# A scaled matmul with an added matrix: rows mapped to tiles in blocks of 1024 in place of one block of 8192

## The chip, the cores and the metric

The kernel runs on one NeuronCore of a Trainium2 chip. The other cores are not used by it. The metric is the device time of one execution in microseconds (us), a median over several runs. The profile is of one execution and reports times from the first to the last instruction (the span), which is shorter than the device time.

## What is computed

```python
# x: (16, 512, 1024) float32, weight: (1024, 768) float32, add_value: (16, 512, 768) float32
def reference(x, weight, scale, add_value):          # scale = 0.1
    return (scale * np.matmul(x, weight) + add_value).astype(np.float32)
```

Flattened, x has 8192 rows of 4 KB, add_value and the output have 8192 rows of 3 KB. The rows are independent of each other, so the kernel may treat them in any order, as long as x, add_value and the output use the same one.

## The kernel before

**Tiles.** The 8192 rows are worked on as 64 tiles of 128 rows, one row in each of the 128 partitions. Which row goes to which tile is set by three views, `x_v`, `add_v` and `out_v` (lines 54 to 56): partition p owns the 64 neighbouring rows 64p to 64p+63, and tile t takes row 64p+t of each partition. One transfer of n tiles therefore reads, in each partition, one unbroken run of n rows (4 KB each for x, 3 KB for add_value and the output); the runs of neighbouring partitions lie 64 rows apart in memory, which is 256 KB for x and 192 KB for the others. The weight has a view of its own, `w_v`: partition p of a transfer takes one 3 KB row, and neighbouring partitions lie two rows, 6 KB, apart.

**The order of transfers.** All transfers are issued by SyncE (SP) in the order of the list `STREAM`, written out by hand. An entry is an operation, a first tile and a number of tiles: `x` loads x (line 241), `w` one of eight weight pieces (line 93), `a` loads add_value (line 247), `o` stores output tiles (line 255), `l` and `r` the left and right part of the last tile. One loop at the end of the kernel walks this list; it also decides when the compute of a tile is recorded, by calling `step()` where a transfer needs room or finished tiles.

**Buffers.** `xs` holds 24 tiles of x (tile t in slot t mod 24). `ao` holds 24 tiles: add_value is loaded into a slot, the result is written over it in place, and the output is stored from it. So `x` of tile t waits until tile t-24 was cast, `o` waits for the last result in it, and `a` of tile t waits until the output of tile t-24 has landed in memory. In the beginning `ao` also holds the weight pieces and the first three products.

**The compute of one tile.** GpSimd (POOL) casts a tile of x to bf16 (line 129). TensorE (PE) transposes it with four matmuls against an identity (line 139), ScalarE (ACT) copies the result out of PSUM (line 145), and PE multiplies it with the eight weight pieces in 16 matmuls (line 161). VectorE (DVE) computes scale times product plus add_value in one instruction (`finish`, line 169). Nine pairs of tiles (`PAIRS`) go another way: GpSimd casts them seven steps ahead (`cast_pair`, line 102), and VectorE transposes them in place of TensorE (`turn_pair`, line 113). Three PSUM buffers (`mm_pool`) take the products, so TensorE can be up to three tiles ahead of VectorE.

**The beginning.** Ten dummy matmuls warm TensorE (line 87). Tiles 0 to 2 are multiplied with the weight pieces as these arrive (`head`); their products are put aside, and add_value is added when it is there (`added`, line 228). Tile 3 is prepared with them, and from tile 4 on the kernel is in its regular course: in `step()` for tile t, four of the eight weight pieces are multiplied, then tile t+1 is transposed, then the other four follow.

Of the kernel before, what the change touches and what calls it, by code (L numbers as in the profile page):

```python
# [11 lines left out]
STREAM = [  # L12
    ("x", 0, 1), ("x", 1, 1), ("x", 2, 1), ("w", 0, 1), ("w", 1, 1), ("w", 2, 1),
    ("w", 3, 1), ("w", 4, 1), ("w", 5, 1), ("x", 3, 1), ("w", 6, 1), ("w", 7, 1),
    ("a", 0, 3), ("x", 4, 4), ("a", 3, 1), ("a", 4, 4), ("x", 8, 4), ("x", 12, 4),
    ("a", 8, 8), ("x", 16, 8), ("a", 16, 8), ("x", 24, 8), ("o", 0, 8), ("o", 8, 8),
    ("a", 24, 4), ("x", 32, 4), ("a", 28, 8), ("a", 36, 4), ("x", 36, 8), ("o", 16, 8),
    ("x", 44, 4), ("a", 40, 8), ("x", 48, 4), ("o", 24, 8), ("x", 52, 8), ("a", 48, 4),
    ("o", 32, 8), ("a", 52, 4), ("a", 56, 8), ("x", 60, 4), ("o", 40, 8), ("o", 48, 8),
    ("o", 56, 4), ("o", 60, 2), ("o", 62, 1), ("l", 63, 1), ("r", 63, 1),  # L20
]

# [10 lines left out]
def kernel(  # L33
# [8 lines left out]
    nc = tc.nc  # L42
    P = 128
# [3 lines left out]
    x_f = x.flatten_outer_dims()  # L47
    add_f = add_value.flatten_outer_dims()
    out_f = out.flatten_outer_dims()
    M, K = x_f.shape  # L50
    _, N = weight.shape
    T = M // P
    KC = K // (2 * P)
    KJ = 2 * KC
    CUT = 512

    x_v = x_f.rearrange("(p t) k -> p t k", p=P)
    add_v = add_f.rearrange("(p t) n -> p t n", p=P)
    out_v = out_f.rearrange("(p t) n -> p t n", p=P)

    w_v = weight.rearrange("(c p r) n -> p c r n", p=P, r=2)

# [10 lines left out]

    zeros = const.tile([P, CUT], bf16, name="zeros")
    nc.vector.memset(zeros, 0.0)  # L75
    identity = const.tile([P, P], fp32, name="identity")
    make_identity(nc, identity)
    xs = const.tile([P, X_SLOTS, K], fp32, name="xs")
    ao = const.tile([P, A_SLOTS, N], fp32, name="ao")
# [6 lines left out]
    for _ in range(WARM):  # L86
        nc.tensor.matmul(warm[:, 0:CUT], zeros[:, 0:P], zeros, start=True, stop=True)  # L87

    def load_w(j, n):

        s = A_SLOTS - KJ + j
        if n == 1:
            nc.sync.dma_start(ao[:, s, :], w_v[:, j // 2, j % 2, :])  # L93
        else:
            nc.sync.dma_start(ao[:, s:s + 2, :], w_v[:, j // 2, :, :])
        for i in range(n):
            nc.vector.tensor_copy(w_bf[:, j + i, :], ao[:, s + i, :])  # L97
# [7 lines left out]
    def turn_pair(t0, a):  # L105

        if a == 0:
            vt = vt_pool.tile([P, 2, KC, P], fp32, tag="vt")
            vt_tiles[t0] = vt
# [23 lines left out]
    def transpose(t, pieces=1):  # L133
        cast_to(t)

        pairs = xb_tiles.pop(t).bitcast(fp32)
        tp = tp_pool.tile([P, KC, P], fp32, tag="tp")
        for c in range(KC):
            nc.tensor.transpose(tp[:, c, :], pairs[:, c * P:(c + 1) * P], identity)  # L139
        xt = xt_pool.tile([P, KJ, P], bf16, tag="xt")  # L140
        src = tp.bitcast(bf16).rearrange("p c (m r) -> p c r m", r=2)
        dst = xt.rearrange("p (c r) m -> p c r m", r=2)
        q = KC // pieces
        for c in range(0, KC, q):
            nc.scalar.copy(dst[:, c:c + q, :, :], src[:, c:c + q, :, :])  # L145
# [18 lines left out]

    BOTH = [(0, CUT), (CUT, N)]

# [8 lines left out]
    def head(op, s, n):  # L175


        for i in range(s, s + n):
            if op == "x" and i < EARLY:
                transpose(i, 2)  # L180
                have_x.append(i)
                for j in have_w:
                    product(i, j, BOTH)
            elif op == "w":
                if i == KJ - 1:
                    transpose(EARLY)
                have_w.append(i)
                for t in have_x:
                    product(t, i, BOTH)
        if len(have_w) == KJ and len(have_x) == EARLY and not done["step"]:  # L190
            for t in range(EARLY):

                if t == 1:
                    nc.scalar.mul(  # L194
                        ao[:, EARLY_AT + t, :], mm_tiles[t, BOTH[0]][:, 0:N], float(scale))
                else:
                    nc.vector.tensor_scalar(  # L197
                        ao[:, EARLY_AT + t, :], mm_tiles[t, BOTH[0]][:, 0:N], float(scale), None,
                        op0=mybir.AluOpType.mult)
            done["step"] = EARLY  # L200
# [3 lines left out]
    def step():  # L204
        t = done["step"]
        if t < T - 1:
            for j in range(KJ):
                if j == KJ // 2:
                    if t + 1 not in in_pair:
                        transpose(t + 1)  # L210
                    cast_to(min(t + 2, done["x"] - 1))
                    if t + 7 in PAIRS:
                        cast_pair(t + 7)
                product(t, j, BOTH)
            finish(t, BOTH[0], 0, N)
            for a in range(P // 32):
                if t + 6 - a in PAIRS:
                    turn_pair(t + 6 - a, a)
        else:
            for cols in BOTH:  # L220
                for j in range(KJ):
                    product(t, j, [cols])
                finish(t, cols, *cols)
        done["step"] += 1

    def added(t):
        assert done["step"] >= EARLY
        nc.vector.tensor_add(  # L228
            ao[:, t, :], ao[:, EARLY_AT + t, :], ao[:, t, :])

    for op, s, n in STREAM:
        last = s + n - 1
        if op == "w":
            load_w(s, n)
            head(op, s, n)
        elif op == "x":
            if last >= X_SLOTS:
                while done["cast"] <= last - X_SLOTS:
                    step()
            k = s % X_SLOTS  # L240
            nc.sync.dma_start(xs[:, k:k + n, :], x_v[:, s:s + n, :])  # L241
            done["x"] = s + n
            if last < EARLY:
                head(op, s, n)
        elif op == "a":
            k = s % A_SLOTS
            nc.sync.dma_start(ao[:, k:k + n, :], add_v[:, s:s + n, :])
            for t in range(s, min(s + n, EARLY)):
                added(t)
        else:  # L250
            while done["step"] <= last:
                step()
            k = s % A_SLOTS
            n0, n1 = {"o": (0, N), "l": (0, CUT), "r": (CUT, N)}[op]
            nc.sync.dma_start(out_v[:, s:s + n, n0:n1], ao[:, k:k + n, n0:n1])


# [33 lines left out]
```

## Time and profile before

| what | value |
|---|---|
| device time, median of 6 runs (lowest to highest) | 212.99 us (212.4 to 213.94) |
| the profiled execution: device time | 213.13 us |
| the profiled execution: span | 211.2 us |
| granted TensorE clock, mean | 0.977 |
| busy share of the span: PE, DVE, POOL, ACT | 93%, 62%, 30%, 23% |
| bytes read from memory, written to it | 61.87 MB, 25.17 MB |

The span and what lies around it (213.13 - 211.2 = 1.9 us) add up to the device time of that execution. A busy share is an average over the whole span; it doesn't say by itself which engine sets the end. For that one has to look at what each waits for, in the stages where it waits. A transfer is seen twice in the profile: the instruction on SP that issues it, and the time from there to its landing, which includes the time that it stands in the queue behind earlier transfers. The 16 DMA engines each carry a sixteenth of every transfer, and a transfer has landed when the last of the 16 is done.

### The profile page before, as it was taken

The numbers are of one execution on the slowest core, as the hardware profiler recorded it, in microseconds if no ns is written. First come the engines' busy times: TensorE is split into PE (matmuls) and PEld (weight loads), VectorE is DVE, ScalarE is ACT, GpSimd is POOL, SyncE is SP. The second block draws the span as 40 slices with busy tenths as digits, with TensorE's granted clock in tenths as the row PEclk, the third lists the DMA queues.
The fourth block names the chain that finished last, engine by engine and source line by source line (L and its number), as shares of the span: only waits on it lengthen the run. The fifth ranks groups of instructions, "written<-read, shape, count | busy, mean of one in ns | idle before, by whom it ended". The sixth has DMA issues, their size and how long they took to land.

```text
span 211.2 us, 3032 instructions
## 1 busy us (share of the span) xinstructions
PE 197.1 (93%) x1218; PEld 120.2 (57%) x1218; DVE 131.2 (62%) x223; ACT 49.2 (23%) x52; POOL 63.8 (30%) x69
## 2 busy tenths in 40 slices
PE   7877299999999999999999999999999999999980
PEld 2544255666566666666565666655666666666650
DVE  1447113229979689699599596986983994223330
ACT  3503013322303103113023031021130230332310
POOL 1310423551080080720900714407208230152000
PEclk9999759999999999999999999999999999999997
DMA  6999999999999999999999999999999999999993
GB/s 237 409 413 446 406 431 428 450 450 394 451 442 399 424 437 433 419 431 427 446 438 420 433 410 447 413 433 447 420 404 440 417 406 436 361 437 441 412 410 118
DMA packets 6781, 87.22 MB, mean 413 GB/s; under 512 B 752, under 2 KB 880, under 8 KB 2928
## 3 DMA queue, kind: packets, MB, share of 16 engines
q1 hardware_dynamic: 6768, 87.03, 97.7%
q8 instruction: 9, 0.15, 0.3%
q14 instruction: 4, 0.03, 0.0%
HBM read 61.87 MB, written 25.17 MB: 412 GB/s over the span
## 4 chain that ended last, share of the span: by engine, by line
PE 85%; DMA 10%; SPq 1%; POOL 0%; ACT 0%; issue 0%; DVE 0%; POOLq 0%; ACTq 0%
PE mm L161 76%; PE tp L139 9%; DMA xs<-in_x_dram 7%; DMA ao<-in_weight_dram 3%; SPq L241 1%; POOL xb L129 0%; ACT xt L145 0%; SPq L93 0%; DVE ao L169 0%; POOLq L129 0%; ACTq L145 0%
## 5 line engine op out<-in xcount | busy, mean ns | idle before, releaser
L161 PE MATMUL mm<-w_bf,xt 128*128 128x512 bf16 (+1 forms) x736 | 130.8, 331 | 1.9 <-DVE w_bf L97 1.3
L161 PEld LDWEIGHTS <-xt 128*128 128x128 bf16 x736 | 69.4, 99 | 52.4 <-ACT xt L145 11.0
L169 DVE SCALAR_TENSOR_TENSOR ao<-mm,ao 128x768 f32<-128x768 f32 (+2 forms) x62 | 58.6, 944 | 60.1 <-PE mm L161 49.8
L145 ACT COPY xt<-tp 128x1024 bf16<-128x1024 bf16 (+1 forms) x49 | 46.5, 963 | 150.3 <-PE tp L139 150.3
L113 DVE STREAM_TRANSPOSE vt<-vx 32x256 f32<-32x256 f32 x144 | 62.7, 436 | 3.1 <-POOL vx L102 0.9
L129 POOL CAST xb<-xs 128x1024 bf16<-128x1024 f32 x43 | 43.6, 1045 | 45.5 <-PE tp L139 24.4
L161 PE MATMUL mm<-w_bf,vt 128*128 128x512 bf16 (+1 forms) x288 | 49.7, 326 | 0.0
L102 POOL CAST vx<-xs 128x1024 bf16<-128x1024 f32 x18 | 18.3, 1043 | 78.8 <-DVE vt L113 43.5
L161 PEld LDWEIGHTS <-vt 128*128 128x128 bf16 x288 | 28.2, 98 | 17.6
L139 PE MATMUL tp<-identity,xb 128*128 128x128 f32 x184 | 28.8, 282 | 5.2 <-POOL xb L129 4.8
L139 PEld LDWEIGHTS tp<-identity,xb 128*128 128x128 f32 x184 | 22.6, 146 | 11.5 <-POOL xb L129 5.2
L97 DVE CAST w_bf<-ao 128x768 bf16<-128x768 f32 x8 | 4.5, 564 | 4.7 <-DMA ao<-in_weight_dram 4.7
L87 PE MATMUL warm<-zeros 128*128 128x512 bf16 x10 | 4.4, 631 | 1.2 <-DVE zeros L75 1.2
L125 DVE CAST xb<-xs 128x512 bf16<-128x512 f32 x3 | 1.3, 427 | 4.9 <-DMA xs<-in_x_dram 4.9
L87 PEld LDWEIGHTS <-zeros 128*128 128x128 bf16 x10 | 1.3, 143 | 3.4 <-issue 2.2
L127 POOL CAST xb<-xs 128x512 bf16<-128x512 f32 x2 | 1.7, 868 | 4.7 <-DMA xs<-in_x_dram 4.7
L228 DVE TENSOR_TENSOR ao<-ao 128x768 f32<-128x768 f32 x3 | 2.7, 951 | 0.0
L197 DVE TENSOR_SCALAR ao<-mm 128x768 f32<-128x768 f32 x2 | 1.8, 952 | 1.0 <-PE mm L161 1.0
L127 ACT ACT_TABLE_LOAD x1 | 1.3, 1283 | 0.7 <-PEq L272 0.7
L127 ACT CAST xb<-xs 128x512 bf16<-128x512 f32 x1 | 0.6, 619 | 2.3 <-DMA xs<-in_x_dram 2.3
L194 ACT ACTIVATE ao<-mm 128x768 f32<-128x768 f32 x1 | 0.8, 816 | 0.0
L75 DVE MEMSET zeros<- 128x256 uint32 x1 | 0.3, 272 | 0.9 <-PEq L272 0.9
(6 smaller groups left out, 0.9 us busy)
## 6 DMA issues: line engine op xcount, KB each, us to landing
out_dram<-ao SPq DMA_DIRECT2D x7, 3072.0 KB, 23.7
xs<-in_x_dram SPq DMA_DIRECT2D x4, 4096.0 KB, 33.5
ao<-in_add_value_dram SPq DMA_DIRECT2D x5, 3072.0 KB, 15.8
xs<-in_x_dram SPq DMA_DIRECT2D x7, 2048.0 KB, 16.9
ao<-in_add_value_dram SPq DMA_DIRECT2D x5, 1536.0 KB, 16.5
ao<-in_weight_dram SPq DMA_DIRECT2D x8, 384.0 KB, 7.4
xs<-in_x_dram SPq DMA_DIRECT2D x4, 512.0 KB, 4.8
out_dram<-ao SPq DMA_DIRECT2D x1, 1536.0 KB, 12.1
```

The costliest lines, as they stand in the source:

```text
L87: nc.tensor.matmul(warm[:, 0:CUT], zeros[:, 0:P], zeros, start=True, stop=True)
L97: nc.vector.tensor_copy(w_bf[:, j + i, :], ao[:, s + i, :])
L102: nc.gpsimd.tensor_copy(vx[:, i, :], xs[:, (t0 + i) % X_SLOTS, :])
L113: nc.vector.transpose(vt[b:b + 32, :, 32 * a:32 * a + 32], pairs[32 * a:32 * a + 32, :, b:b + 32])
L127: other(xb[:, K // 2:K], src[:, K // 2:K])
L129: nc.gpsimd.tensor_copy(xb, src)
L139: nc.tensor.transpose(tp[:, c, :], pairs[:, c * P:(c + 1) * P], identity)
L145: nc.scalar.copy(dst[:, c:c + q, :, :], src[:, c:c + q, :, :])
L161: nc.tensor.matmul(mm_tiles[t, cols[0]][:, n0:n1], lhs(t, j), w_bf[:, j, n0:n1], start=(j == 0), stop=(j == KJ - 1))
L169: nc.vector.scalar_tensor_tensor(a, mm_tiles[t, part][:, n0:n1], float(scale), a, op0=mybir.AluOpType.mult, op1=mybir.AluOpType.add)
L228: nc.vector.tensor_add(ao[:, t, :], ao[:, EARLY_AT + t, :], ao[:, t, :])
L241: nc.sync.dma_start(xs[:, k:k + n, :], x_v[:, s:s + n, :])
```

## The change

Three things change. First, the views: rows are grouped in 8 blocks of 1024. In a block, partition p owns 8 neighbouring rows, and tile t of the 64 takes row `1024*(t//8) + 8*p + t%8`. A transfer of 8 tiles covers one unbroken stretch of memory (4 MB of x, 3 MB of the others); one of 4 tiles reads or writes half of each partition's 8 rows. Inside a partition the run is as long as before for the same number of tiles. Neighbouring partitions now lie 32 KB (x) and 24 KB (the others) apart.

Second, a helper `rows` picks a block and tiles in it, and refuses a transfer that crosses a block's border. Third, since some entries of `STREAM` crossed such borders, the list is written anew: where transfers of 8 tiles began at a tile that is not a multiple of 8, they are moved or split, and the order around them differs. The number of entries, 47, and the bytes are the same.

```diff
 STREAM = [
     ("x", 0, 1), ("x", 1, 1), ("x", 2, 1), ("w", 0, 1), ("w", 1, 1), ("w", 2, 1),
     ("w", 3, 1), ("w", 4, 1), ("w", 5, 1), ("x", 3, 1), ("w", 6, 1), ("w", 7, 1),
-    ("a", 0, 3), ("x", 4, 4), ("a", 3, 1), ("a", 4, 4), ("x", 8, 4), ("x", 12, 4),
-    ("a", 8, 8), ("x", 16, 8), ("a", 16, 8), ("x", 24, 8), ("o", 0, 8), ("o", 8, 8),
-    ("a", 24, 4), ("x", 32, 4), ("a", 28, 8), ("a", 36, 4), ("x", 36, 8), ("o", 16, 8),
-    ("x", 44, 4), ("a", 40, 8), ("x", 48, 4), ("o", 24, 8), ("x", 52, 8), ("a", 48, 4),
-    ("o", 32, 8), ("a", 52, 4), ("a", 56, 8), ("x", 60, 4), ("o", 40, 8), ("o", 48, 8),
+    ("a", 0, 3), ("a", 3, 1), ("x", 4, 4), ("x", 8, 4), ("a", 4, 4), ("x", 12, 4),
+    ("a", 8, 8), ("x", 16, 8), ("a", 16, 8), ("x", 24, 8), ("o", 0, 8), ("x", 32, 8),
+    ("a", 24, 4), ("a", 28, 4), ("o", 8, 8), ("x", 40, 4), ("a", 32, 8), ("o", 16, 8),
+    ("x", 44, 4), ("a", 40, 8), ("x", 48, 4), ("o", 24, 8), ("x", 52, 4), ("a", 48, 8),
+    ("x", 56, 4), ("o", 32, 8), ("x", 60, 4), ("a", 56, 8), ("o", 40, 8), ("o", 48, 8),
     ("o", 56, 4), ("o", 60, 2), ("o", 62, 1), ("l", 63, 1), ("r", 63, 1),
 ]
...
-    x_v = x_f.rearrange("(p t) k -> p t k", p=P)
-    add_v = add_f.rearrange("(p t) n -> p t n", p=P)
-    out_v = out_f.rearrange("(p t) n -> p t n", p=P)
+    G = 8
+
+    x_v = x_f.rearrange("(g p t) k -> p g t k", p=P, t=G)
+    add_v = add_f.rearrange("(g p t) n -> p g t n", p=P, t=G)
+    out_v = out_f.rearrange("(g p t) n -> p g t n", p=P, t=G)
+
+    def rows(view, s, n):
+        assert s // G == (s + n - 1) // G
+        return view[:, s // G, s % G:s % G + n, :]
...
-            nc.sync.dma_start(xs[:, k:k + n, :], x_v[:, s:s + n, :])
+            nc.sync.dma_start(xs[:, k:k + n, :], rows(x_v, s, n))
...
-            nc.sync.dma_start(ao[:, k:k + n, :], add_v[:, s:s + n, :])
+            nc.sync.dma_start(ao[:, k:k + n, :], rows(add_v, s, n))
...
-            nc.sync.dma_start(out_v[:, s:s + n, n0:n1], ao[:, k:k + n, n0:n1])
+            nc.sync.dma_start(rows(out_v, s, n)[:, :, n0:n1], ao[:, k:k + n, n0:n1])
```

The instructions on TensorE, VectorE, ScalarE and GpSimd are the same in kind, number and order; what differs there is which transfers they wait for.

## The prediction, made before the changed kernel ran

> **What bounds the kernel now.** I read the chain of waits first, then the DMA rows, then the stages one by one, because the first two seem to contradict each other. The page gives:
>
> ```profile
> DMA  6999999999999999999999999999999999999993
> GB/s 237 409 413 446 406 431 428 450 450 394 451 442 399 424 437 433 419 431 427 446 438 420 433 410 447 413 433 447 420 404 440 417 406 436 361 437 441 412 410 118
> q1 hardware_dynamic: 6768, 87.03, 97.7%
> PE 85%; DMA 10%; SPq 1%; POOL 0%; ACT 0%; issue 0%; DVE 0%; POOLq 0%; ACTq 0%
> ```
>
> The chain puts 85% on PE, yet the data queue keeps the 16 DMA engines busy for 97.7% of the span. The chain in order of time shows where each rules:
>
> ```profile
> 9.81 13.85 DMA xs<-in_x_dram
> ...
> 23.80 1.05 POOL xb L129
> ...
> 24.90 1.12 PE tp L139 x4
> 26.02 5.08 PE mm L161 x16
> ...
> 31.53 2.63 PE mm L161 x16
> ...
> 205.41 0.42 DVE ao L169
> ```
>
> The transfer of x tiles 4 to 7, issued at 9.81 and landed 13.85 later (23.66), frees GpSimd's cast and then PE at 24.90. From there PE runs almost without a hole until 205.4; the first tile takes 5.08 us, later ones 2.63 plus 0.44 of transposes. But the chain follows the last engine instruction, which ends at 205.8, and the span goes on to 211.2. The last 5.4 us belong to the output transfers. The stages in between, each row being busy times, then granted PE clock, DMA share, GB/s:
>
> ```profile
> 8.00:13.00 5.00, 4.84 (x31) 2.76 (x30) 2.88 (x6) 1.56 (x4) 0.00 (x0) 1.00 1.03 404
> 29.00:73.00 44.00, 44.00 (x281) 27.17 (x279) 27.74 (x47) 12.14 (x12) 13.10 (x13) 0.98 1.00 429
> 182.00:184.50 2.50, 2.50 (x18) 1.61 (x17) 0.39 (x2) 1.01 (x1) 0.00 (x0) 1.00 1.09 347
> 188.00:203.00 15.00, 15.00 (x99) 9.32 (x98) 4.44 (x6) 5.06 (x5) 3.27 (x4) 1.00 0.99 421
> 207.00:208.20 1.20, 0.00 (x0) 0.00 (x0) 0.00 (x0) 0.00 (x0) 0.00 (x0) 1.00 0.39 143
> 208.20:210.40 2.20, 0.00 (x0) 0.00 (x0) 0.00 (x0) 0.00 (x0) 0.00 (x0) 0.55 0.05 20
> ```
>
> The DMA engines are full from the first bytes to about 207. In the last 2.2 us they move at 20 GB/s with a share of 0.05, about one engine of 16: one straggler finishes alone, 2.2 us after the others. The end is set by the transfer stream, and in it by its slowest engine. PE stands just behind: the last store is issued at 205.87, the 15 other engines are through at about 208.1 (the 1.2 us from 207 at a mean share of 0.39), so 2.3 us pass from the last issue to their end, and PE could be about 2.2 us later before the straggler at 210.3 ceased to hide it.
>
> **What the Trainium skill says.** The page "DMA: Bandwidth & Descriptors", section "Bandwidth", puts the ceiling of the 16 engines' path at 435 GB/s; the trace's 429 in the stretch from 29 to 73 us agrees, and leaves 1.4%. "HBM Reference", section "Specifications (TRN2)", says that a core that streams alone is bounded by its 16 DMA engines at about 425 GB/s rather than by the memory; 429 agrees. "DMA: Bandwidth & Descriptors", section "Latency and other measured facts", says that the distance of the partitions' rows matters when it is a large power of two: full rate at 512 KiB, less at 2 MiB, and that contiguous tiles are a cure. The trace has 256 KB (x) and 192 KB at full rate, so it agrees that there is nothing to cure here. "TensorE: Matmul & The Clock Gate", section "Part 1: The HAM clock gate", says that an idle window of about 3.4 us halves the clock until one window was busy; the trace agrees, with 5.08 us for the first tile after a wait of 4.8.
>
> **The change, part by part.**
>
> *Dense stretches.* Each partition's run stays n rows long, so the DMA engines carry the same runs; only the distance between runs shrinks. The profile holds a near test: weight pieces, 384 KB in 3 KB rows 6 KB apart, and add_value tile 3, also 384 KB in 3 KB rows, 192 KB apart. The casts that wait for the weight pieces:
>
> ```profile
> 8.84 0.56 DVE L97 CAST w_bf<-ao 128x768 bf16<-128x768 f32 x1 [0.42 <-DMA ao<-in_weight_dram]
> 9.81 0.56 DVE L97 CAST w_bf<-ao 128x768 bf16<-128x768 f32 x1 [0.41 <-DMA ao<-in_weight_dram]
> ```
>
> and the landing of tile 3 of add_value (KB, us from issue):
>
> ```profile
> ao<-in_add_value_dram SPq DMA_DIRECT2D x1, 384.0 KB, 13.8
> ```
>
> A weight piece takes 0.97 us, 393,216 bytes at 405 GB/s. Tile 3 was issued at 10.79 and landed 13.8 later, at 24.6; the transfer ahead of it had landed at 23.66, so it took 0.93 to 0.98. Rows 6 KB and 192 KB apart cost the same within 5%. The bounds: at best the whole stream goes to 435 GB/s. From 23.66 to 203 the data stream averages 75.4 MB in 179.4 us, 420 GB/s, so at the ceiling 6 us less, which PE doesn't allow (rival 1); at worst the crowded addresses cost something that no row shows. I take 0, since the long stretch at 429 leaves little, and the one visible stall (182 to 184.5) has no known tie to the distance.
>
> *Sizes.* x has twelve 4 and 8 tile transfers after the change and eleven before (one 8 is split: 128 runs more); add_value has three of 4 and six of 8 tiles, for five and five (128 runs fewer in sum). These cancel: 0.
>
> *Beginning.* Tile 3 of add_value now precedes x tiles 4 to 7. It took 0.93 to 0.98 us, so these land at about 24.6 in place of 23.66, and PE starts 0.9 us later. If the clock is still released at 31 us, fewer half-speed microseconds are worked and half of the delay returns; I take 0.5 to 0.9. PE ends at 206.3 to 206.7. The last store then clears the 15 engines at about 205.87 + 0.9 + 2.3 = 209.1 at latest, still ahead of the straggler's 210.3. Cost now: 0; without the straggler it would show in full.
>
> *The new order in the middle.* I add up landings (named by the entry's letter and first tile) from x tiles 24 to 31, which keep their place and landed at 27.83 + 45.5 = 73.3. Differences of landings before give 3.7 us for 1.5 MB, 4.85 for 2 MB, 7.3 for 3 MB, 9.7 for 4 MB. After: o0 80.6, x32 90.3, a24 94.0, a28 97.7, o8 105.0, x40 109.9, a32 117.2, o16 124.5, x44 129.3, a40 136.6, x48 141.5, o24 148.8, x52 153.6, a48 160.9, x56 165.8, o32 173.1, x60 177.9, a56 185.2, o40 192.5, o48 199.8. Before, o48 was issued at 182.28 and landed 20.7 later, at 203.0: by then the straggler had lost 3.2 us over this sum, so late entries may be up to 3 us later.
> Against the need: VectorE's `finish` of tile 24 was at 91.8, of 32 at 115.1, of 40 at 137.7, of 48 at 162.9 and of 56 at 184.4; add 0.9. Then a24 is 1.3 us late, a32 1.2 us, a40 and a48 are in time, a56 0 to 3 us late. Behind each late `finish` stand VectorE's turns and later finishes. Three PSUM buffers cover it: a finish holds up PE only when it is more than two tiles, about 5.3 us, less its own 0.96, behind. None is. x comes earlier than before (x32 90.3 against 81.19 + 15.3 = 96.5; tiles 52 to 55 at 153.6), so GpSimd and the turns gain slack.
>
> *Waits of SP.* Each `a` from tile 24 on waits for a store to land. In the new order a single 2 MB x transfer stands behind that store at four places (a32, a40, a48, a56). It keeps the queue filled for 4.85 us, less the lag of the last engine (about 2.2) that the wait includes; 2.6 are left. Before, a56 had only a 1.5 MB transfer as cover (3.7 less 2.2), and the stream went on with at most a small dip. So 0, and even a dip hits the leading engines, not the straggler. Stores up to o40 find VectorE's results ready when SP comes to them (o40 is reached at 173, tile 47's `finish` was at 158.6), so they hold back no load.
>
> The sum is 213.13 (span 211.2) plus 0. The profiled execution stands 0.14 above the median of the six runs, so the forecast for the median is 213.0.
>
> **Rivals.**
> 1. The stalls come from the spread addresses and vanish. For it: x tiles 60 to 63 landed at 170.5 + 16.5 = 187.0, 6.0 us after a56 (181.0), where 4.85 is normal; the 347 GB/s lie there. Against it: the same kind of transfer ran at full rate elsewhere. It gives at least 1.1 us; beyond that PE is the floor, 209.1 + 0.9 (from the last landing to the end of the span now, 211.2 - 210.3) + 1.9 = 211.9.
> 2. The other side: the dense stretches are slower. The 16 engines now work within 4 MB, and if they meet in the same part of the memory, each run takes longer. The price is direct, as the stream is full for 206 us: 2% would be 4.1 us, 217.1. It decides from 0.5%, 1.1 us. For it: no row shows 16 or 32 KB runs this close. Against it: the weights' rows and the skill's page.
> 3. The change does what it says but SP's four waits with little cover each open 1 us for all engines: the first 2 us are taken from the leaders' lead, 2 remain, 215.0. Against it: 2.6 us of cover.
> 4. PE is held: x or `a` late by over 4.3 us, or the cold clock lasts one window longer (1.7 us at half speed). It costs only past 2.2 us of delay; 2.5 + 0.9 late gives 214.2.
>
> **How the numbers follow.** The forecast of no change has 0.6 (its own range 212.0 to 214.0), rival 1 0.2, rival 2 0.12, rivals 3 and 4 0.04 each. About 0.5% is what a measurement of this kernel can tell from no change, so faster 0.2 (below 211.9), within 0.6, slower 0.2 (above 214.05). The range reaches to 211.5, below rival 1's floor by half a PE delay, and to 215.0, rivals 3 and 4; it leaves out rival 2.
>
> **What would show it.** Right: the stretch 29 to 73 us stays at 427 to 431 GB/s, PE's first transpose of the regular course comes at 25.6 to 25.9, add_value waits of VectorE grow by a few us without a hole in PE, and the tail again shows one or two engines. Wrong: a different GB/s in that stretch (rival 2 if lower), no lone engine at the end and no slow stretch (rival 1), DMA digits below 9 in the middle (rival 3), PE waiting after 35 us (rival 4).

## The result, and the profile after

| | median of runs | ratio to before (95% interval) |
|---|---|---|
| before | 213.22 us | |
| after | 212.08 us | 0.9953 (0.9936 to 0.997) |

The change makes the kernel faster by 0.47%, about 1.0 us: within the half per cent that was called no change, but clear of zero with this many runs. The middle half of the runs went from 212.6 to 214.2 before to 211.8 to 212.4 after, so it is also steadier. A ratio, here and below, leaves out the runs that lie over 1.5% above the fastest of their kernel; medians and ranges are of all runs. The profiled execution after took 212.03 us with a span of 210.3.

The page of the kernel after, the lines that answer to those of before (DMA share in 40 slices, GB/s in them, the data queue, the chain by engine):

```profile
DMA  6999999999999999999999999999999999999994
GB/s 226 409 415 437 424 416 435 455 446 421 393 468 438 402 441 444 397 414 444 415 429 405 425 427 444 410 438 435 415 443 418 439 408 438 430 421 433 423 388 185
q1 hardware_dynamic: 6768, 87.03, 98.1%
PE 85%; DMA 10%; SPq 1%; POOL 1%; ACT 0%; issue 0%; DVE 0%; POOLq 0%; ACTq 0%
```

The packets and bytes are the same, 6768 and 87.03 MB. The chain has nearly the same shares. The slice that stood out before, 361 GB/s near 182 us, is gone; between the first slice and the last none is under 388. The chain in order of time after (start, us, what):

```profile
10.98 13.82 DMA xs<-in_x_dram
...
24.94 1.05 POOL xb L136
...
26.04 1.11 PE tp L146 x4
27.15 5.07 PE mm L168 x16
```

x tiles 4 to 7 land at 24.80 in place of 23.66, and TensorE begins 1.14 us later, at 26.04 in place of 24.90. The first tile again runs at half clock, 5.07 us. So TensorE became later, and yet the kernel ends earlier. The stages (busy times, then granted PE clock, DMA share, GB/s):

```profile
29.00:73.00 44.00, 44.00 (x276) 26.91 (x275) 27.20 (x47) 12.14 (x12) 13.16 (x13) 0.97 1.00 429
...
182.00:184.50 2.50, 2.50 (x18) 1.54 (x17) 0.96 (x1) 0.44 (x2) 0.48 (x2) 1.00 1.01 403
207.00:208.20 1.20, 0.00 (x0) 0.00 (x0) 0.00 (x0) 0.00 (x0) 0.00 (x0) 1.00 0.81 300
208.20:210.40 2.20, 0.00 (x0) 0.00 (x0) 0.00 (x0) 0.00 (x0) 0.00 (x0) 0.80 0.08 27
```

From 29 to 73 us the rate is 429 GB/s, to the digit as before: in that part of the stream dense stretches are worth nothing. Two things differ late. From 182 to 184.5 it is 403 instead of 347, and the tail is shorter: the engines work together until 208.2 (share 0.81 where it was 0.39) and little is left after that. But from 23.66 us, where x tiles 4 to 7 land in the kernel before, to 203 us the two executions move the same, the kernel before in the first line, the kernel after in the second:

```profile
23.66:203.00 179.34, 177.93 (x1122) 109.66 (x1123) 118.84 (x204) 42.50 (x42) 60.30 (x60) 0.98 1.01 427
23.66:203.00 179.34, 176.78 (x1116) 109.04 (x1117) 118.40 (x203) 41.81 (x42) 60.40 (x60) 0.98 1.00 427
```

What the later one gains in a short stretch, it has lost elsewhere by 203 us, and in this pair the span's 0.9 us come from the tail. One pair of profiles doesn't settle the cause; the experiments have to.

### The profile page after: what moved, and what is told of

Same layout as the page of the kernel before. It is cut to its first block, busy times and chain, and to the rows that moved or that the text cites. A ratio compares the mean times of both kernels' runs of the same rounds, so it can differ in the third digit from the quotient of the medians.

```text
span 210.3 us, 3034 instructions
## 1 busy us (share of the span) xinstructions
PE 196.5 (93%) x1218; PEld 119.3 (57%) x1218; DVE 130.9 (62%) x223; ACT 49.4 (23%) x52; POOL 63.9 (30%) x69
## 3 DMA queue, kind: packets, MB, share of 16 engines
q1 hardware_dynamic: 6768, 87.03, 98.1%
## 4 chain that ended last, share of the span: by engine, by line
PE 85%; DMA 10%; SPq 1%; POOL 1%; ACT 0%; issue 0%; DVE 0%; POOLq 0%; ACTq 0%
PE mm L168 76%; PE tp L146 9%; DMA xs<-in_x_dram 7%; DMA ao<-in_weight_dram 3%; SPq L100 1%; SPq L248 1%; POOL xb L136 1%; ACT xt L152 0%; DVE ao L176 0%; POOLq L136 0%; ACTq L152 0%
## 5 line engine op out<-in xcount | busy, mean ns | idle before, releaser
L146 PEld LDWEIGHTS tp<-identity,xb 128*128 128x128 f32 x184 | 21.7, 142 | 13.5 <-POOL xb L136 6.2
```

## The experiments

Three things had changed at once: the views, the order after tile 24, and the order at the beginning. The theories: (A) the layout spares slow packets; (B) the order mends a hole; (C) TensorE's later begin sets the new end. A view of 15.5 us, from 169 to 184.5 us, turned out to sort the orders, so I show it first: what the data stream moved there, in the kernel before,

```profile
DMA packets 383, 6.29 MB, mean 406 GB/s; under 512 B 38, under 2 KB 38, under 8 KB 38
```

and in the kernel after:

```profile
DMA packets 344, 6.54 MB, mean 422 GB/s; under 512 B 35, under 2 KB 35, under 8 KB 35
```

0.25 MB more at about 430 GB/s are worth 0.6 us in this stretch; that they reach the end of the kernel is not shown by the pair.

### Order and layout apart

New order, old views: `e1` is the kernel before with the new `STREAM`. Old order, dense views: `e2` is the kernel after with

```diff
-    ... ("a", 28, 8), ("a", 36, 4), ("x", 36, 8) ... ("x", 52, 8) ...
+    ... ("a", 28, 4), ("a", 32, 4), ("a", 36, 4), ("x", 36, 4), ("x", 40, 4) ... ("x", 52, 4), ("x", 56, 4) ...
```

in the old list; `e3` is this split list with the old views.

> The new STREAM with the old views (each partition owns 64 neighbouring rows, so transfers read spread runs). If the dense layout made the gain, this stays at the time before, ratio 0.998 to 1.003, and its end is set by a lone DMA engine. If the new order made it, the ratio is about 0.995, as in the changed kernel. PE begins its regular course at about 26.0 us as in the changed kernel in either case.

> The dense views with the old order of STREAM, where the three transfers that cross a block's border (add_value 28 to 35, x 36 to 43, x 52 to 59) are split into two of 4 tiles. If the dense layout made the gain, the ratio is about 0.993 to 0.996, better than the changed kernel by up to 0.9 us, since PE begins at 24.9 us again. If the order made it, the ratio is about 1.0.

> Control for the split: the kernel before with the same three transfers split, old views. Both theories expect 1.0 within 0.002; the three extra issues cost SP under half a us each and lie behind queued transfers.

Measured: e1 0.9964 (0.9932 to 0.9995), middle half 211.8 to 213.4 us; e2 0.9972 (0.9945 to 0.9998), 212.4 to 213.6; e3 0.998 (0.9951 to 1.0008), 212.3 to 215.0. The order alone gives most of the gain; the layout alone, e2 against e3, 0.08%, which these intervals can't tell from nothing. The stretch from 169 to 184.5 us in e2, dense views and old order:

```profile
DMA packets 389, 6.27 MB, mean 405 GB/s; under 512 B 42, under 2 KB 42, under 8 KB 42
```

It is as poor as before with its spread views, and the slow 2.5 us in it are there too:

```profile
182.00:184.50 2.50, 2.50 (x18) 1.49 (x17) 0.69 (x1) 1.01 (x1) 0.00 (x0) 1.00 1.04 315
```

So theory A falls for this stretch: 315 GB/s with dense x. e3 (old order, old views) has 405 in the whole stretch as well, e1 (new order, old views) 425. The stretch follows the order.

### The hole before add_value 56

The old order has `("o", 32, 8), ("a", 52, 4), ("a", 56, 8), ("x", 60, 4)`. The load of add_value 56 waits until the store of tiles 32 to 39 has landed on its last engine, and only 1.5 MB are queued behind that store. In the kernel before, at that place:

```profile
170.00:171.00 1.00, 1.00 (x8) 0.61 (x7) 0.97 (x3) 0.00 (x0) 0.00 (x0) 1.00 0.93 385
171.00:172.00 1.00, 1.00 (x9) 0.81 (x8) 0.99 (x2) 0.22 (x1) 0.18 (x1) 1.00 1.24 418
```

The share drops to 0.93, then it is 1.24 at 418 GB/s: the packets after the gap take longer than their bytes need. `e5` exchanges two entries of the kernel before, nothing else:

```diff
-    ("a", 56, 8), ("x", 60, 4), ("o", 40, 8)
+    ("x", 60, 4), ("a", 56, 8), ("o", 40, 8)
```

> The kernel before with one pair of entries exchanged: x tiles 60 to 63 go ahead of add_value tiles 56 to 63. In the kernel before, the load of add_value 56 waits for a store to land and has only a 1.5 MB transfer queued behind that store, so the leading DMA engines stand idle for about 1 us near 170 us, one of them perhaps the one that ends last. If this hole is what the new order mended, this is faster than before by 0.5 to 1.0 us (ratio 0.995 to 0.998) and the leading engines show no loss there. If the order gains elsewhere, the ratio is 1.0.

Measured: 0.994 (0.9902 to 0.9979), an interval that holds the change's 0.9953. The same places in e5:

```profile
170.00:171.00 1.00, 1.00 (x9) 0.79 (x8) 0.97 (x3) 0.24 (x1) 0.20 (x1) 1.00 1.01 418
171.00:172.00 1.00, 1.00 (x7) 0.50 (x6) 0.99 (x2) 0.77 (x1) 0.84 (x1) 1.00 1.00 426
182.00:184.50 2.50, 2.50 (x18) 1.42 (x16) 0.00 (x0) 1.01 (x1) 1.04 (x1) 1.00 0.93 393
```

and over the 15.5 us:

```profile
DMA packets 402, 6.66 MB, mean 430 GB/s; under 512 B 41, under 2 KB 41, under 8 KB 41
```

No dip, no swollen share, 0.37 MB more than before, which is 0.9 us. (A microsecond holds one or two packets of each engine, so single microseconds scatter between profiles; the sum over 15.5 us is the safer reading.) The slow 2.5 us at 182 have gone with the hole, although x has the old view. How the two hang together stays open; the exchange removes both. The tie is not a strict one: e12 below, with the new order and dense views, has 344 GB/s from 182 to 184.5 us, although 2 MB stand behind the store there.

The counterpart, `e6`, makes a hole in the kernel after:

```diff
-    ("x", 56, 4), ("o", 32, 8), ("x", 60, 4), ("a", 56, 8)
+    ("x", 56, 4), ("x", 60, 4), ("o", 32, 8), ("a", 56, 8)
```

> The changed kernel with x tiles 60 to 63 moved ahead of the store of tiles 32 to 39, so that nothing stands in the queue behind this store when the load of add_value 56 waits for its landing. If a wait with too little cover empties the DMA engines and what they lose is not made up, all engines lose about 2 us there and the time goes up by 1.5 to 3 us over the changed kernel (ratio to before 1.002 to 1.010). If the stream has slack against TensorE, it stays at 0.995 to 0.998.

Measured: 1.0138 (1.0093 to 1.0184), 1.9% above the kernel after, which is 4 us and more than expected. The place:

```profile
176.00:178.40 2.40, 2.40 (x16) 1.46 (x15) 0.96 (x1) 0.00 (x0) 0.00 (x0) 1.00 0.27 113
178.40:179.00 0.60, 0.60 (x6) 0.35 (x4) 0.39 (x1) 0.00 (x0) 0.00 (x0) 1.00 0.00 0
179.00:180.00 1.00, 1.00 (x9) 0.74 (x8) 0.56 (x1) 0.00 (x0) 0.00 (x0) 1.00 1.42 344
180.00:181.00 1.00, 1.00 (x8) 0.62 (x7) 0.00 (x0) 0.60 (x1) 0.56 (x1) 1.00 0.24 98
181.00:182.00 1.00, 1.00 (x7) 0.51 (x6) 0.36 (x1) 0.41 (x1) 0.48 (x1) 1.00 1.20 516
```

From 176 the leading engines run dry one by one, from 178.4 to 179 nothing moves, and then the first packets take so long that the share reads 1.42 at 344 GB/s. Added up, 1.23 MB moved in 6 us where 2.58 would at 430 GB/s: 3.1 us lost. This hole cost the wait for the last engine, the time from issue to data, and a slow start on top.

### The layout by itself

To see the layout without TensorE, these kernels hold only the transfers of the new order; the compute is left out.

> The transfers of the new STREAM alone with the old views; all compute is left out, so the output is add_value's bytes. It measures the stream without TensorE. If the dense layout spares the DMA engines slow packets, this is slower than the same with dense views by 0.5 to 1 us in the median and more so in its upper quarter; if not, the two agree within 0.2 us. Both should lie near 205 to 208 us.

> The transfers of the new STREAM alone with the dense views; all compute is left out, so the output is add_value's bytes. See the run with the old views: faster than it by 0.5 to 1 us if the layout matters to the DMA engines, equal within 0.2 us if not.

Measured: spread 0.9927 (0.9897 to 0.9956), dense 0.9785 (0.974 to 0.9831). By itself the layout is worth 1.4%, about 3 us, more than was expected, though both lie above the 205 to 208 us that were expected. The six dense runs also scatter less than the 22 spread ones, 208.7 to 209.2 us against 210.6 to 218.3. Which tensor does it? `e9` has dense x and spread add_value and output, `e10` the reverse, `e11` blocks of 32 tiles for all, `e13` and `e15` other distances for x, with the rest dense:

```diff
-    x_v = x_f.rearrange("(g p t) k -> p g t k", p=P, t=G)
+    x_v = x_f.rearrange("(g p t) k -> p g t k", p=P, t=64)
...
+    x_v = x_f[0:60 * P].rearrange("(g p t) k -> p g t k", p=P, t=60)
...
+    x_v = x_f.rearrange("(g p t) k -> p g t k", p=P, t=16)
```

These are e10, e13 and e15 in turn.

> The transfers of the new STREAM alone, all compute left out, x with the dense view, add_value and output with the old one (partitions 192 KB apart). If the slow stretches come from x, whose partitions lie 256 KB apart in the old view, this is as steady as the all-dense stream, 208.7 to 209.2 us. If they come from add_value and the output, it is as slow and as spread out as the all-spread stream, median 211 to 213.

> The counterpart: x with the old view (256 KB apart), add_value and output dense, all compute left out. Slow and spread out (211 to 213) if x is the cause, near 209 if add_value and the output are.

> The transfers of the new STREAM alone, all compute left out, with blocks of 4096 rows: 32 neighbouring rows for each partition, so partitions lie 128 KB (x) and 96 KB (the others) apart, and a transfer of 8 tiles is not dense but covers a quarter of a block. If it takes one dense stretch to avoid slow packets, this is like the old views, median 211 to 213. If a lesser distance is enough, it lies near 209.

> The transfers of the new STREAM alone, all compute left out, add_value and output dense, x with 60 rows for each partition, so partitions lie 240 KB apart in place of 256; the last x transfer reads tiles 56 to 59 a second time and rows past 7680 of x are left out. If x is slow because its distance is a power of two, this is steady at 208.7 to 209.5 us. If any spread of that size is slow, it is like the run with x 256 KB apart, 210 to 216.

> The transfers of the new STREAM alone, all compute left out, add_value and output dense, x in blocks of 16 tiles, so partitions lie 64 KB apart and a transfer of 8 tiles covers half of each run. It tells how much of the distance is needed: steady at 209 if 64 KB is still near enough, 210 to 216 if only a dense stretch helps.

| x: distance of partitions | add_value and output | ratio to before (95% interval) | runs in the ratio | lowest to highest, us |
|---|---|---|---|---|
| 32 KB (e8) | 24 KB | 0.9785 (0.974 to 0.9831) | 6 of 6 | 208.66 to 209.19 |
| 32 KB (e9) | 192 KB | 0.9798 (0.9741 to 0.9855) | 6 of 6 | 208.74 to 210.87 |
| 64 KB (e15) | 24 KB | 0.9829 (0.979 to 0.9869) | 6 of 6 | 209.33 to 209.82 |
| 128 KB (e11) | 96 KB | 0.9857 (0.9778 to 0.9936) | 3 of 6 | 209.23 to 217.15 |
| 240 KB (e13) | 24 KB | 0.9914 (0.9884 to 0.9945) | 18 of 22 | 210.05 to 217.49 |
| 256 KB (e10) | 24 KB | 0.9885 (0.9813 to 0.9957) | 3 of 6 | 210.29 to 216.17 |
| 256 KB (e7) | 192 KB | 0.9927 (0.9897 to 0.9956) | 16 of 22 | 210.61 to 218.25 |

It is x: five of the six runs of e9 lie below all of e10, taken beside them, though the two intervals meet. 192 KB for the others does no harm that shows. A power of two is not needed, since 240 KB is slow too, with an interval clear of that at 64 KB, taken beside it. The prediction leant on the Trainium skill's page "DMA: Bandwidth & Descriptors", section "Latency and other measured facts", which has copies with a distance of 512 KiB at 207 GB/s, close to the 214 that it calls full; in this mixed stream 256 KB costs 1%, and the measurement decides. A transfer need not be dense: 64 KB is near enough. 128 KB is open: only the scatter speaks, and the interval reaches both sides. e8 to e11 and e15 have six runs each, too few to show how far they scatter. Why such distances hurt x and not add_value stays open.

Where the time goes shows in e10, x spread and the rest dense (stretch and length, POOL busy, clock, DMA share, GB/s):

```profile
29.00:73.00 44.00, 0.00 (x0) 1.00 1.01 432
112.00:116.00 4.00, 0.00 (x0) 1.00 0.99 381
137.00:141.00 4.00, 0.00 (x0) 1.00 1.04 371
```

and in e8, all dense:

```profile
29.00:73.00 44.00, 0.00 (x0) 1.00 1.01 431
112.00:116.00 4.00, 0.00 (x0) 1.00 0.98 418
137.00:141.00 4.00, 0.00 (x0) 1.00 1.05 449
```

The share is as full in both; with x spread it moves fewer bytes in a few stretches. These stretches come when stores are in the stream (from 73 us on); in the 44 us before, both run at 431 or 432. These two stretches are picked; over the whole time from 23.66 to 203 us it is 426 GB/s in e10 and 430 in e8.

### Does TensorE set the new end?

`e4` puts x tiles 4 to 7 ahead of add_value tile 3 again; `e12` also fills TensorE's wait for them:

```diff
+                    if t == EARLY:
+                        fill = mm_pool.tile([P, 1024], fp32, tag="mm")
+                        for _ in range(18):
+                            nc.tensor.matmul(
+                                fill[:, 0:CUT], zeros[:, 0:P], zeros, start=True, stop=True)
```

> The changed kernel with x tiles 4 to 7 ahead of tile 3 of add_value again, as before. If PE, begun 1.1 us later, sets the end of the changed kernel, this is faster than it by 0.6 to 1.1 us: ratio to the kernel before about 0.990 to 0.992. If the DMA stream still sets the end, it stays at 0.995.

> The changed kernel with x tiles 4 to 7 first (as in e4), and 18 dummy matmuls that keep TensorE busy while it waits for them, so that its clock stays up and the first tile of the regular course takes about 2.7 us in place of 5.1; TensorE ends about 2.4 us earlier. If TensorE sets the end of e4, this is faster by 0.5 us or more, ratio to before about 0.990. If the DMA stream with its last engine does, it equals e4, 0.993 to 0.994.

Measured: e4 0.9936 (0.9913 to 0.996), e12 0.9933 (0.9894 to 0.9973). That looked like a third of a us from TensorE's begin (0.9953 to 0.9936), and nothing more from a fast first tile. Because these runs and those of the kernel after were not taken side by side, I put e4 beside it once more, and e5 too.

> The changed kernel once more, beside e17 and e18 on the same chip, so that the three can be compared: 211.6 to 212.4 us for its middle half, ratio about 0.995.

> The changed kernel with x tiles 4 to 7 ahead of tile 3 of add_value, once more. If the changed kernel's median is set by TensorE's later begin, this is 0.3 to 0.9 us below it and as steady; if not, equal to it within 0.2 us.

> The kernel before with one exchange (x 60 to 63 ahead of add_value 56), old views, once more. If the spread view of x costs the full kernel only now and then, its lowest times equal e17's and its upper quarter is 0.5 us or more above e17's.

Measured on one chip: the kernel after 212.25 us, 0.9952 (0.9931 to 0.9973); with x first 212.41 us, 0.9966 (0.9942 to 0.999); the one exchange in the kernel before 211.85 us, 0.9928 (0.9903 to 0.9953), middle half 211.4 to 212.3. The gain of e4 did not come back, so theory C falls: TensorE's begin is not what sets the end, the transfers still do. A gain of under half a us is not excluded, for the two limits lie close: the last store, 128 KB, landed 4.5 us after its issue in the kernel before and 2.4 us in the kernel after. And the one exchange, with the old views, gives all that the change gave. Its interval overlaps that of the kernel after, so that it is better, by 0.2%, isn't shown. Its upper quarter begins at 212.3 us and that of e17 at 212.6, so the cost of spread x that was looked for there doesn't show in the full kernel.

Last, the exchange and the dense views together in the old order:

> Dense views with the old order (the three crossing transfers split) and x tiles 60 to 63 ahead of add_value 56 to 63. If the dense x and the hole before add_value 56 are all that the change gained by, this has both and is at the changed kernel's time or, with TensorE begun earlier, up to 0.8 us below: ratio 0.991 to 0.995, and as steady. If the new order holds something more, it stays near 0.997.

Measured: 0.9965 (0.9944 to 0.9987), 212.21 us, middle half 212.1 to 212.5, not side by side with the last three. It was expected at 0.991 to 0.995, and near 0.997 if the new order holds something more; it is nearer the latter. Beside e2, the same kernel without the exchange (0.9972), it gains 0.07%, nothing that these intervals show (medians 212.21 and 212.87 us, on different chips), though the stretch from 169 to 184.5 us went from 405 to 432 GB/s. So the gain of the exchange is shown with the old views alone, and why it doesn't show with the dense ones stays open.

Over all twelve profiles of whole kernels other than e6, this stretch has 405 or 406 GB/s in the three with the old order and 418 to 432 in the nine with the new order or the exchange, whichever views they have. It sorts the orders, then, but doesn't tell how long one execution takes: the profiled ones of e14 (432 GB/s) and e18 (429) took 212.95 and 213.13 us, and that of the kernel before (406) 213.13.

## Why the prediction was wrong

The forecast was 213.0 us and no change; the measured median is 212.08, and the ratio is clear of 1. The mechanism was seen right, a full stream with its last engines setting the end and TensorE just behind, and the range held. What failed is one term of the sum.

- *Waits of SP: this is the step that failed.* The prediction counted four waits of the new order and asked whether they would open holes. They didn't. It saw the wait of the old order too, the load of add_value 56 with 3.7 us of cover less 2.2, but passed over it as "at most a small dip" and set the gain from its removal at 0. As a gap it is small indeed, a share of 0.93 in one microsecond. It is not free: the packets right after it are slow (a share of 1.24 for 418 GB/s), the slow 2.5 us at 182 (347 GB/s) come and go with it in the old order, and the exchange that removes it measured 0.994 and 0.9928 (e5, e18), where the sum had no gain. Over the stretch e5 moves 0.9 us' worth more. The prediction's second guard, that a dip hits only the leading engines and so costs nothing, fell too; that engines which lead at 170 us need their lead for later delays is my reading, and no run shows it by itself.
- *Dense stretches: 0.* For the kernel as a whole nothing else is shown: 0.1% between e2 and e3, and between e1 and the kernel after. The reason given was only half right. The rate of the long undisturbed stretch and the pair of 384 KB transfers told that the distance costs nothing at the beginning; they couldn't tell of stretches beside stores, and the stream by itself loses 3 us. The bound is too wide as well: 420 GB/s from 23.66 to 203 us counts landings of the last engine, while the engines moved 427 there, so that the ceiling leaves 3 us and not 6. A small near test early in the run doesn't stand for a stage with other traffic.
- *Rival 1* had the right amount (211.9 us) and the right place (182 to 184.5), and the wrong cause: those slow packets are there with dense views too (e2), so the spread addresses don't make them. That its figure came out is luck. *Rivals 2, 3 and 4* didn't happen: 429 GB/s from 29 to 73 us; no hole in the new order; TensorE without a hole after the beginning.
- *Beginning.* Predicted 0.9 us later, with up to half of it back; measured 1.14 at TensorE's begin, and none back, since the half clock again held for the whole first tile (5.07 us). Hidden, as predicted: the last store is issued at 207.0 instead of 205.87, and the span is shorter all the same.
- *The new order in the middle.* The sums held. VectorE's add of tile 24 was predicted 1.3 us late and that of tile 32 1.2 us late against 92.7 and 116.0; they began at 94.34 and 117.90:

```profile
94.34 0.96 DVE L176 SCALAR_TENSOR_TENSOR ao<-mm,ao 128x768 f32<-128x768 f32 x1 [1.68 <-PE tp L146]
```

```profile
117.90 1.89 DVE L176 SCALAR_TENSOR_TENSOR ao<-mm,ao 128x768 f32<-128x768 f32 x2 [1.99 <-DMA ao<-in_add_value_dram]
```

  Three PSUM buffers covered both, as was said: no wait of TensorE came of it. Tiles 48 to 55 of the output were predicted to land at 199.8 to 202.8; issued at 183.42 and 18.6 later, they landed at 202.0.

## What to carry to other kernels

Where a load waits for a store to land, add up what stands in the queue behind that store: it must last for the lag of the last DMA engine and for the time from issue to data (here 3.7 us of cover left a dip, 4.85 us did not, and with none the stream lost 3.1 us). Look for such places in the old version of a change too; what a rewrite mends by the way may be all of its gain. A rate in a stretch of one profile is a pointer; whether it reaches the end, only the times of many runs tell. Measure a layout in the stream alone before judging it in a kernel where other waits hide it.

## What the runs showed of the hardware

- A queue that runs empty costs more than the gap: around 0.6 us in which no packet began, 3.1 us of stream were lost in 6 us. The engines had run dry one by one before, and afterwards the first microsecond moved 344 GB/s and the second 98 (e6).
- Loads of x with partitions 256 KB apart ran at full rate as long as no store was in the stream (432 GB/s from 29 to 73 us), and at 371 and 381 GB/s in two stretches of 4 us with stores; at 32 KB the same stretches had 449 and 418 (e10, e8). At 240 KB the stream is slower as well (0.9914, e13) and at 64 KB hardly (0.9829, e15); add_value and the output at 192 KB did no harm that shows (e9).
